# Low weight parts staged in DRAM, memory scores one unit ahead, and state space products in one pass of stacked parts

## The chip, the core and the metric

The kernel runs on one core of a Trainium2 chip. The metric is the device time of one execution in microseconds; before the change it is 2162.36 us (median of 3 runs, 2160.61 to 2164.85). A core has a matmul engine (TensorE: PE, and PEld for its weight loads), VectorE (DVE), ScalarE (ACT), GpSimd (POOL) and SyncE (SP), which here only issues DMAs. Each engine works through its own list of instructions in the order of that list, and waits on semaphores for the others; DMAs are issued from the lists of SP, ACT and POOL.

## The reference

A sequence of 512 tokens of width 1024, float32, goes through two blocks: a dilated window attention and a differential attention, each with gate and output projection; then a feed-forward network (gate and up projections of 2816, hidden product, output), a mixing layer, and a second feed-forward network. The mixing layer is where most of the change lies:

```python
q_a, k_a, v_a, q_i, k_i, w_i, u_s, q_m, gates = jnp.split(h @ w_in, offsets, axis=-1)
o_a = indexed_sparse_attention(q_a, k_a, v_a, ...) @ w_o_a      # top 128 of 512 keys per query
y_s = gelu(s5_layer(u_s, ...))                                  # 16 groups x 64 complex states
o_b = glu_a * sigmoid(glu_b)          # of y_s @ w_glu
o_m = memory_attention(q_m, m_k, m_v) @ w_o_m                   # 4 heads, 256 memory rows
g = sigmoid(gates)
x = x + (g[0] * o_a + g[1] * o_b + g[2] * o_m) @ w_out
```

The state space layer needs `bur = B_re u`, `bui = B_im u` per group (its input products), a complex linear recurrence over the 512 tokens, and `y = Re(C x) + d u`.

## The kernel before

**Weights.** All weight matrices are streamed as pieces of 128x1024 float32 (512 KB or less) through one plan, `self.plan`. A piece is loaded by SP (`_load`, L291, tile `raw`, 2 buffers), then split (`_split` L305, `split` L174): ACT casts it to the matmul's one-pass format (`wh`, L175) and DVE subtracts that from the original (`wl`, L176), the low part. A product is three one-pass matmuls, high x high, low x high and high x low (`mm3`, L151, lines L153 to L155), which together keep float32 accuracy. Split pieces have 4 buffers and are split up to three pieces ahead of use. Two shapes of loops use them: `tok` (L335, tokens on the output's partitions) and `feat` (L384, features there). Both accumulate in the four PSUM banks `pp`; a `tok` of four token tiles or a `feat` of 512 columns takes all four, so the next one can begin only when the first bank has been read out. In the feed-forward network (`ffn`, L908) the reading out of the output projection is the DVE addition `xa<-pp` (L1656).

**The order of the work.** The program is emitted by a planner that counts PE time in `self.clock`: side work is written as generators that `yield` a number of planner microseconds or a condition, and `pump` (L111) emits what is due between matmuls. Its `yield`s are guesses. What is emitted is then placed by a scheduler of the framework, engine by engine, by dependencies and its own idea of durations, so an instruction can move ahead of others that were emitted earlier. On the chip the lists that come out are fixed.

**Preparation.** While the first feed-forward runs, `prepare` (L1355) normalises the memory rows, and `s5_setup` (L966) computes the rotation tables of the state space: eight rounds on POOL (L1065 to L1067, tiles `s5cs` and `s5t`, which share the buffers `memx0` and `memx1` of the memory rows), each ended by a store to DRAM from POOL's DMA queue (L1068, `s5tab<-s5cs`). `bias_table` (L1174) makes a row `brow` (buffer `gmem`) that POOL stores as `btab`.

**Mixing.** `mix` (L1385) adds the steps: key, value and index projections, memory queries (`qm`), state space input (`us`, `ev_us` L1451), queries (`q`), then gate and output projections of the three branches (`branch`, L1498). Beside them run as generators the index search (`index_masks`, L1232, 16 rounds of MAX8 and MATCH_REPLACE8 on DVE per query tile), sparse attention (`sparse_attn`, L1267, tiles `bm`, `apt`), memory attention (`mem_attn`, L1191) and the state space (`s5_branch`, L1091). Their matmuls use plain float32 (`mm`, L158, line L159), transposes L164, PSUM banks `pa`.

Memory attention has eight units (4 token tiles x 2 pairs of heads). A unit computes scores (`pa<-mkT,qmT`), a masked row maximum on DVE and an exponential on ACT (L437, L438, tile `msm`), waits 4 planner us, transposes the probabilities (`pa<-cst,msm`) and multiplies by the values (`pa<-mv,mpt`). The next unit begins after that.

The state space has eight units too. POOL masks the input matrix to a block diagonal form (`bz`, L1125), PE transposes it, two float32 products with `us` follow (`pa<-us,bt`), then DVE and POOL rotate, scan along the tokens and rotate back (L1138 to L1154, ending with `s5t` L1153 and `s5wi` L1154); 10 planner us later PE reads them (`pa<-s5t,cz`, `pa<-s5wi,cz`).

Of the kernel before, what the change touches and what calls it, by code (L numbers as in the profile page):

```python
# [9 lines left out]
F32 = mybir.dt.float32  # L10
FR = mybir.dt.float32r
# [3 lines left out]
OP = mybir.AluOpType  # L15
# [4 lines left out]
P = 128  # L20
D = 1024
S = 512
NT = S // P
# [3 lines left out]
RAW, RING, AHEAD = 2, 4, 2  # L27
RQ = 2

S5GAP, SPGAP = 10.0, 2.5  # L30
# [35 lines left out]
class Net:  # L66
    def __init__(self, ctx, tc, consts):
        self.tc, self.nc = tc, tc.nc
        pool = lambda name, bufs, **kw: ctx.enter_context(tc.tile_pool(name=name, bufs=bufs, **kw))
        self.open = lambda c, name, bufs: c.enter_context(tc.tile_pool(name=name, bufs=bufs, reuse_waits="tile"))  # L70
        self.consts = consts
        self.cpool = pool("consts", 1)
        self.rings = {"u": pool("u", 2), "y": pool("y", 2)}
        self.wraw = pool("wraw", RAW)
        self.wsplit = pool("wsplit", RING)
        self.small = pool("small", 2)
        self.pp = pool("pp", 4, space=PSUM)
        self.pa = pool("pa", 4, space=PSUM)
        self.dram = pool("dram", 1, space=DRAM)
        self.flip = self.open_xn = 0  # L80
        self.spare_dve = False
        self.clock, self.seq, self.heap = 0.0, 0, []
        self.steps, self.plan = [], []
        self.raws, self.ready, self.live = [], {}, 0


# [204 lines left out]
    def _load(self):  # L291
# [11 lines left out]
        self.raws.append(raw)  # L303

    def _split(self):  # L305
        i = self.next_split
        raw = self.raws[i]
        n, nk = raw.shape[2], raw.shape[1]
        h, l = (self.wsplit.tile([P, 1024], FR, name="w" + x, tag="w" + x)[:, :nk * n]
                .rearrange("p (k c) -> p k c", k=nk) for x in "hl")  # L310
        self.split(raw, h, l)
        self.ready[i] = [(h[:, j, :], l[:, j, :]) for j in range(nk)]
# [778 lines left out]
    def s5_branch(self, a, us, tmp, act, dst):  # L1091
# [7 lines left out]
        tabs = []  # L1099

        def fetch(q):
            cs = tmp.tile([P, 2, S], F32, name="s5cs", tag="cs", bufs=2)
            nc.scalar.dma_start(cs, self.s5tab[q])
            tabs.append(cs)

        fetch(0)
        for ft in range(2):
# [10 lines left out]
            for qq in range(4):  # L1118
# [3 lines left out]
                bz = tmp.tile([P, 2, P], F32, name="bz", tag="bz")  # L1122
                cz = tmp.tile([P, 2, P], F32, name="cz", tag="cz")
                for i in range(2):
                    G.tensor_tensor(bz[:, i, :].rearrange("p (b c) -> p b c", c=16),  # L1125
                                    bb[:, i, q, :].unsqueeze(1).to_broadcast([P, 8, 16]), m48[:, qq], op=OP.mult)
                G.tensor_tensor(cz, ct, m4[:, qq, :].unsqueeze(1).to_broadcast([P, 2, P]), op=OP.mult)
                yield S5LEAD
                b = self.bank()
                for i in range(2):  # L1130
                    self.T(b[:, i * P:(i + 1) * P], bz[:, i, :])
                bt = tmp.tile([P, 2, P], F32, name="bt", tag="bt")
                self.evac(bt.rearrange("p i c -> p (i c)"), b[:, :2 * P])
                br, bi = self.bank(), self.bank()
                self.mm(br, bt[:, 0, :], us[:, ft, :])
                self.mm(bi, bt[:, 1, :], us[:, ft, :])
                C, Sn = (tabs[q][:, i, :] for i in range(2))
# [22 lines left out]
                nc.scalar.copy(y[rows, :], yp[rows, :])  # L1160
            yield 1.5
            t = tmp.tile([P, S], F32, name="gt", tag="t2")
            V.scalar_tensor_tensor(y, us[:, ft, :], dc[:, ft:ft + 1], y, op0=OP.mult, op1=OP.add)
            G.tensor_tensor(t, y, y, op=OP.mult)
# [25 lines left out]

    def mem_attn(self, qT, kT, v, act, at, st, bm):  # L1191
        nc = self.nc
        for t in range(NT):
            nm = st.tile([P, 4], F32, name="mnm", tag="mnm")
            den = st.tile([P, 4], F32, name="mden", tag="mden")
            o = at.tile([P, 4, 64], F32, name="mo", tag="kk", bufs=1)
            for j in range(2):
                yield bm.free
                held = bm.take()
                sm = at.tile([P, 2, 256], F32, name="msm", tag="bm", bufs=bm.n)  # L1200
                b = [self.bank()[:, :256] for _ in range(2)]
                for c in range(2):
                    hs = slice(c * 64, c * 64 + 64)
                    self.mm(b[c], qT[hs, j, t * P:(t + 1) * P], kT[hs, j, :])
                for c in range(2):
                    hd = 2 * j + c
                    self.softmax_rows(b[c], self.dm[:, :256], sm[:, c, :], nm[:, hd:hd + 1], den[:, hd:hd + 1])
                yield MEM[0]
                tb = self.bank()
                pt = at.tile([P, 4, P], F32, name="mpt", tag="apt", bufs=2)  # L1210
                for n in range(4):
                    self.T(tb[:, n * P:(n + 1) * P], sm[:, n // 2, (n % 2) * P:(n % 2 + 1) * P])
                held[0] = True
                self.evac(pt.rearrange("p n q -> p (n q)"), tb)
                po = self.bank()[:, :P]
                for c in range(2):
                    hd = 2 * j + c
                    for kt in range(2):
                        self.mm(po[:, c * 64:c * 64 + 64], pt[:, 2 * c + kt, :], v[:, kt, hd * 64:hd * 64 + 64],
                                kt == 0, kt == 1)  # L1220
                d = den[:, 2 * j:2 * j + 2]
                nc.vector.reciprocal(d, d)
                nc.vector.tensor_tensor(o[:, 2 * j:2 * j + 2, :], po.rearrange("p (h d) -> p h d", h=2),
                                        d.unsqueeze(2).to_broadcast([P, 2, 64]), op=OP.mult)
            b = self.bank()
# [3 lines left out]
            act.done.add(t)  # L1229
            yield MEM[1]  # L1230

# [123 lines left out]
    def prepare(self, a, pre, aux):  # L1355
# [15 lines left out]
        def gen():  # L1371
# [8 lines left out]
            yield 5.0  # L1380
            v["btab"] = self.bias_table(a["rel_bias"], a["onehot"], aux)

        self.co(gen())

    def mix(self, u, a, enter, merged):  # L1385
# [10 lines left out]
        def opened():  # L1396
# [7 lines left out]
            tl("qaT", [P, 4, S]), tl("kaT", [P, S]), tl("ixT", [P, 3, S]), tl("va", [P, NT, 64])  # L1404
            tl("wi", [P, NT, 4]), tl("us", [P, 2, S])
            v["M"] = [mx.tile([P, S], F32, name="M%d" % f) for f in range(KT)]
# [44 lines left out]
        def ev_us(c, ps, _):  # L1451
            self.evac(v["us"][:, c, :], ps[c])
            flags["us"].add(c)
# [37 lines left out]

        self.tok(ux, [(w, 1220, 256)], ev_heads("qm", 4, "qmT", 2), by="t")
        self.feat(ux, [(w, 964, 256)], ev_us)
        self.add(start_s5)
# [62 lines left out]
        branch(2, om, a["w_o_m"], True, False)  # L1557
        branch(1, ys, a["w_glu"], False, False)

        def leave():  # L1560
# [17 lines left out]
    def run(self, a, out):  # L1578
# [107 lines left out]
        def enter_mix():  # L1686
            self.need(lambda: len(self.mixv["mk"]) == 2)
            s3.close()
            return s2
# [122 lines left out]
```

## Time and profile before

| | |
|---|---|
| median of 3 runs | 2162.36 us (2160.61 to 2164.85) |
| profiled execution | 2165.69 us, its span 2163.9 us |
| PE busy | 2103.0 us (97%) |
| PEld busy | 1709.3 us (79%) |
| DVE busy | 1237.9 us (57%) |
| ACT busy | 938.7 us (43%) |
| POOL busy | 234.5 us (11%) |
| DMA | 204.11 MB, mean 94 GB/s |

The profile gives for each engine the time in which an instruction of it ran. PE's matmuls are pipelined: one 128x512 matmul shows some 0.39 us, but the next starts 0.23 us after it. Stages differ, so the shares of the whole span say little; the windows below cut it into stretches. The first feed-forward's weights are loaded from about 930 to 1294 us, the mixing layer's from 1327 to 1762 us. An idle stretch of an engine is shown with what ended it, and PEclk is the share of TensorE's clock that was granted.

### The profile page before, as it was taken

To read this page: it belongs to the slowest core of one execution; us is meant where nothing else is said; L and a number is where in the kernel's file an instruction comes from. 1 tells how busy PE (TensorE), PEld (TensorE's weight loads), DVE (VectorE), ACT (ScalarE), POOL (GpSimd) and SP (SyncE) were. 2 spreads that over 40 slices of the span, in tenths; PEclk is the share of its full clock that TensorE was granted. 3 is DMA by queue.
4 is the path that set the end of the run, shared out by engine and by line. 5 is a ranking of instruction groups with operands and counts; after the bars stand their busy time and mean duration, and the time that the engine had idled before them with its cause. 6 is when DMAs were issued, how large, how long until landed. Compare 5 with 4: busy or idle time off the path is not lost.

```text
span 2163.9 us, 27643 instructions
## 1 busy us (share of the span) xinstructions
PE 2103.0 (97%) x10217; PEld 1709.3 (79%) x10217; DVE 1237.9 (57%) x2673; ACT 938.7 (43%) x1885; POOL 234.5 (11%) x322
## 2 busy tenths in 40 slices
PE   7999999999999999999999999988899999999998
PEld 6888988889888776788888888755567888888887
DVE  5645457454667677876543337889885454333334
ACT  4746455464545655555223234433344234223223
POOL 0000000000000000110970000124431100000000
PEclk9999999999999999999999999989999999999999
DMA  5222222212233212233343334222243323333332
GB/s 176 88 69 69 69 70 63 83 59 69 80 127 127 88 59 69 98 120 109 117 146 98 98 98 154 79 60 74 64 143 97 110 81 99 97 97 98 98 98 78
DMA packets 152055, 204.11 MB, mean 94 GB/s; under 512 B 9848, under 2 KB 111240, under 8 KB 151920
## 3 DMA queue, kind: packets, MB, share of 16 engines
q1 hardware_dynamic: 138368, 170.70, 25.8%
q10 hardware_dynamic: 8352, 15.14, 2.4%
q0 software_dynamic: 5200, 16.50, 2.1%
q8 instruction: 80, 1.31, 0.3%
q14 instruction: 55, 0.45, 0.1%
HBM read 191.80 MB, written 10.51 MB: 93 GB/s over the span
## 4 chain that ended last, share of the span: by engine, by line
PE 49%; DVE 8%; ACT 2%; DMA 1%; issue 1%; POOL 1%; ACTq 0%; DVEq 0%; POOLq 0%; SPq 0%
PE pp L153 15%; PE pp L154 15%; PE pp L155 15%; PE pa L159 3%; PE pa L164 1%; DVE wl L176 1%; DVE s5wi L1148 1%; DVE score L1262 1%; DVE s5wr L1147 1%; DMA raw<-in_w_in 1%; ACT wh L175 1%; DVE s5t L1150 0%; ACT p L438 0%; DVE m L1261 0%; POOL s5wr L1142 0%
## 5 line engine op out<-in xcount | busy, mean ns | idle before, releaser
L176 DVE TENSOR_TENSOR wl<-raw,wh 128x1024 fp32r<-128x1024 f32 (+1 forms) x320 | 410.4, 1283 | 496.1 <-ACT wh L175 494.9
L175 ACT CAST wh<-raw 128x1024 fp32r<-128x1024 f32 (+1 forms) x320 | 333.7, 1044 | 636.8 <-PE pp L154 287.5
L153 PE MATMUL pp<-uh,wh 128*128 128x512 f32 (+1 forms) x1232 | 485.0, 394 | 0.2 <-DVE sg L445 0.2
L154 PE MATMUL pp<-ul,wh 128*128 128x512 f32 (+1 forms) x1232 | 478.2, 388 | 1.0 <-DVE ul L282 1.0
L155 PE MATMUL pp<-uh,wl 128*128 128x512 f32 (+1 forms) x1232 | 477.5, 388 | 0.0
L153 PEld LDWEIGHTS pp<-uh,wh 128*128 128x128 f32 x1232 | 232.0, 189 | 54.4 <-issue 9.9
L155 PEld LDWEIGHTS pp<-uh,wl 128*128 128x128 f32 x1232 | 232.4, 189 | 46.0 <-issue 0.6
L154 PEld LDWEIGHTS pp<-ul,wh 128*128 128x128 f32 x1232 | 233.0, 189 | 43.7 <-DVE ul L282 1.2
L153 PE MATMUL pp<-wh,uh 128*128 128x512 f32 (+2 forms) x592 | 237.9, 403 | 0.3 <-ACT wh L175 0.2
L154 PE MATMUL pp<-wl,uh 128*128 128x512 f32 (+2 forms) x592 | 229.2, 388 | 0.5 <-DVE wl L176 0.4
L155 PE MATMUL pp<-wh,ul 128*128 128x512 f32 (+2 forms) x592 | 228.6, 387 | 0.0
L153 PE MATMUL pp<-yh,wh 128*128 128x512 f32 (+1 forms) x464 | 176.0, 379 | 0.0
L154 PE MATMUL pp<-yl,wh 128*128 128x512 f32 (+1 forms) x464 | 175.1, 377 | 0.0
L155 PE MATMUL pp<-yh,wl 128*128 128x512 f32 (+1 forms) x464 | 174.8, 377 | 0.0
L425 ACT COPY rq<-pp 32x512 f32<-32x512 f32 x256 | 148.0, 578 | 58.0 <-PE pp L155 52.8
L153 PEld LDWEIGHTS pp<-wh,uh 128*128 128x128 f32 x592 | 127.8, 216 | 21.2 <-issue 4.6
L154 PEld LDWEIGHTS pp<-wl,uh 128*128 128x128 f32 x592 | 128.3, 217 | 17.3 <-DVE wl L176 1.8
L155 PEld LDWEIGHTS pp<-wh,ul 128*128 128x128 f32 x592 | 127.6, 215 | 16.6 <-issue 0.3
L153 PE MATMUL pp<-wh,yh 128*128 128x512 f32 x304 | 119.2, 392 | 0.1
L154 PE MATMUL pp<-wl,yh 128*128 128x512 f32 x304 | 118.8, 391 | 0.0
L155 PE MATMUL pp<-wh,yl 128*128 128x512 f32 x304 | 118.6, 390 | 0.0
L438 ACT ACTIVATE sm<-sm,nm 128x128 f32<-128x128 f32 (+1 forms) x192 | 79.8, 417 | 54.4 <-DVE nm L437 54.1
(404 smaller groups left out, 2774.4 us busy)
## 6 DMA issues: line engine op xcount, KB each, us to landing
raw<-in_ffn_w_in SPq DMA_DIRECT2D x176, 256.0 KB, 3.1
raw<-in_dil_w_in SPq DMA_DIRECT2D x80, 512.0 KB, 3.6
raw<-in_ffn_w_out SPq DMA_DIRECT2D x44, 512.0 KB, 3.7
raw<-in_diff_w_in SPq DMA_DIRECT2D x32, 512.0 KB, 3.7
raw<-in_w_in SPq DMA_DIRECT2D x32, 512.0 KB, 3.7
raw<-in_dil_w_out SPq DMA_DIRECT2D x8, 512.0 KB, 3.7
raw<-in_diff_w_out SPq DMA_DIRECT2D x8, 512.0 KB, 3.6
s5tab<-s5cs POOLq DMA_DIRECT2D x8, 512.0 KB, 3.3
```

Of the source, the lines that this page charges most:

```text
L153: mm(ps, a[0], b[0], start=first, stop=False)
L154: mm(ps, a[0], b[1], start=False, stop=False)
L155: mm(ps, a[1], b[0], start=False, stop=last)
L159: self.nc.tensor.matmul(ps, a, b, start=start, stop=stop)
L164: self.nc.tensor.transpose(ps, x, self.ident[:n, :n])
L175: self.nc.scalar.copy(h, src)
L176: return self.nc.vector.tensor_tensor(l, src, h.bitcast(F32), op=OP.subtract)
L425: nc.scalar.copy(sw[b:b + 32, :], ps[c][b ^ 32:(b ^ 32) + 32, :])
L438: nc.scalar.activation(sm, sm, AF.Exp, bias=nm, scale=-1.0, accum_out=den)
L1147: V.tensor_tensor_scan(wr, mag, wr, 0.0, op0=OP.mult, op1=OP.add)
L1148: V.tensor_tensor_scan(wi, mag, wi, 0.0, op0=OP.mult, op1=OP.add)
L1262: V.match_replace(sc[:, :n], m8, sc[:, :n], -BIG)
```

## The change

Three parts.

**Staging.** After the bias table and a lead of `ELEAD` = 95 planner us, a new generator `low_parts` takes the plan's pieces from the state space input on, up to the end of the second branch. For each it loads the raw weights from POOL's queue into `wr0` (the buffers `memx0` and `gmem` in turn), splits them with ACT and DVE as `_split` does (the high part goes to `wh0` in `memx1`, one buffer, and isn't kept; the low part replaces the raw data), and POOL stores the low part to DRAM (`low`). When mixing begins (`early_on` false) it stops; 21 pieces have been staged by then, 4 of them of half size. In mixing, `_split` of a staged piece casts the high part on ACT as before, and SP loads the low part instead of DVE's subtraction.

**Memory attention.** The scores of unit n + 1 are emitted before the transposes and the values of unit n; the yields become 2 and 2 planner us.

**State space input.** `us` is split into a high and a low part, which are stored to DRAM; each unit loads the 32 rows that it needs, high and low twice, stacked into 128 partitions (`u4`, four DMAs on ACT's queue). The input matrix of a unit (tile `bf`, 128x32 for real and imaginary part) is split into high and low as well, and copied by POOL into a matrix whose rows 0 to 63 hold the high part twice and 64 to 127 the low part twice (`bz`). One one-pass matmul of 128 rows then sums all four products of parts. At the end of a half the two parts of `us` are loaded again for `d u`, one addition each.

How the instructions move, in three places. First DVE, in the first feed-forward, around the copies of the bias row (`wl` is a piece's ordinary subtraction, `xa` the reading out of the output projection, `wr` a staged piece's subtraction). Before:

```order
L176 TENSOR_TENSOR wl<-raw,wh 128x1024
L1186 COPY brow<-pa 8x512
L1186 COPY brow<-pa 8x128
L176 TENSOR_TENSOR wl<-raw,wh 128x1024 x3
L1656 SCALAR_TENSOR_TENSOR xa_7835<-pp,xa_7835 128x512
L1656 SCALAR_TENSOR_TENSOR xa_7836<-pp,xa_7836 128x512
L1656 SCALAR_TENSOR_TENSOR xa_7837<-pp,xa_7837 128x512
L1656 SCALAR_TENSOR_TENSOR xa_7838<-pp,xa_7838 128x512
L176 TENSOR_TENSOR wl<-raw,wh 128x1024 x4
```

Now:

```order
L1244 COPY brow<-pa 8x512
L1244 COPY brow<-pa 8x128
L178 TENSOR_TENSOR wl<-raw,wh 128x1024 x2
L178 TENSOR_TENSOR wr_10008<-wr_10008,wh_10040 128x1024
L178 TENSOR_TENSOR wr_10043<-wr_10043,wh_10109 128x1024
L178 TENSOR_TENSOR wl<-raw,wh 128x1024
L1745 SCALAR_TENSOR_TENSOR xa_7835<-pp,xa_7835 128x512
L1745 SCALAR_TENSOR_TENSOR xa_7836<-pp,xa_7836 128x512
L1745 SCALAR_TENSOR_TENSOR xa_7837<-pp,xa_7837 128x512
L1745 SCALAR_TENSOR_TENSOR xa_7838<-pp,xa_7838 128x512
L178 TENSOR_TENSOR wr_10112<-wr_10112,wh_10158 128x1024
L178 TENSOR_TENSOR wl<-raw,wh 128x1024
```

The first two staged subtractions stand ahead of the third ordinary one and of the four additions; a third follows the additions. On ACT the casts of the same pieces stand in the same places among the ordinary casts.

Then POOL, the last table of the state space and what follows it. Before:

```order
L1066 TENSOR_TENSOR s5t<-e_8867,e_8868 128x512 x2
L1188 DMA btab<-brow 8x640
L1065 TENSOR_TENSOR s5cs<-e_8867,e_8868 128x512 x2
L1067 TENSOR_TENSOR s5cs<-s5cs,s5t 128x512 x2
L1068 DMA s5tab<-s5cs 128x1024
L1668 DMA x_82<-xa_7835 128x1024
L1668 DMA x_82<-xa_7836 128x1024
L1668 DMA x_82<-xa_7837 128x1024
```

Now:

```order
L1104 TENSOR_TENSOR s5t<-e_8867,e_8868 128x512 x2
L1246 DMA btab<-brow 8x640
L1103 TENSOR_TENSOR s5cs<-e_8867,e_8868 128x512 x2
L1105 TENSOR_TENSOR s5cs<-s5cs,s5t 128x512 x2
L1106 DMA s5tab<-s5cs 128x1024
L319 DMA wr_10043<-in_w_in 128x4x256
L319 DMA wr_10008<-in_w_in 128x4x256
L335 DMA low<-wr_10008 128x1024
L335 DMA low<-wr_10043 128x1024
L319 DMA wr_10112<-in_w_in 128x2x512
L319 DMA wr_10161<-in_w_in 128x2x512
L335 DMA low<-wr_10112 128x1024
```

The list up to the last store of a table is unchanged; the loads and stores of the staging come between it and the stores of `xa`.

Last PE, in mixing, around the products of the first state space unit (`bt` its matrix, `msm` the probabilities of a memory unit, `mkT,qmT` the scores). Before:

```order
L159 MATMUL pa<-us,bt 128x512 x2
L164 MATMUL pa<-cst,msm 128x128 x4
L153 MATMUL pp<-wh,uh 128x512
L154 MATMUL pp<-wl,uh 128x512
L155 MATMUL pp<-wh,ul 128x512
L153 MATMUL pp<-wh,uh 128x512
L159 MATMUL pa<-mv,mpt 128x64 x4
L159 MATMUL pa<-mkT,qmT 128x256 x2
```

Now:

```order
L1189 MATMUL pa<-u_11973,bt 128x512 x2
L161 MATMUL pa<-mkT,qmT 128x256 x2
L157 MATMUL pp<-wh,ul 128x512
L155 MATMUL pp<-wh,uh 128x512
L156 MATMUL pp<-wl,uh 128x512
L157 MATMUL pp<-wh,ul 128x512
L155 MATMUL pp<-wh,uh 128x512
L166 MATMUL pa<-cst,msm 128x128 x4
L156 MATMUL pp<-wl,uh 128x512
```

The scores of the second memory unit stand ahead of the transposes of the first unit's probabilities, with other matmuls between; before they came behind the first unit's values.

The diff, cut to its core (in `mem_attn` the old body is left out, and the new helpers hold the same instructions as it):

```diff
+EGAP, ELEAD = 5.0, 95.0
...
+        self.low, self.early, self.early_on = {}, (0, 0), True
...
+    def low_parts(self, pool):
+        nc = self.nc
+        yield ELEAD
+        tags = ("memx0", "gmem")
+        def load(i):
+            parts, k0, nk = self.plan[i]
+            n = sum(p[2] for p in parts)
+            r = pool.tile([P, D], F32, name="wr0", tag=tags[i % 2])[:, :nk * n].rearrange("p (k c) -> p k c", k=nk)
+            o = 0
+            for w, c0, m in parts:
+                nc.gpsimd.dma_start(r[:, :, o:o + m],
+                                    w[k0 * P:(k0 + nk) * P, c0:c0 + m].rearrange("(k p) c -> p k c", p=P))
+                o += m
+            return r
+        r = load(self.early[0])
+        for i in range(*self.early):
+            yield EGAP
+            if not self.early_on:
+                return
+            nk, n = r.shape[1], r.shape[2]
+            h = pool.tile([P, D], F32, name="wh0", tag="memx1")[:, :nk * n].rearrange("p (k c) -> p k c", k=nk)
+            self.split(r, h.bitcast(FR), r.bitcast(FR))
+            nxt = load(i + 1) if i + 1 < self.early[1] else None
+            yield EGAP / 2
+            low = self.dram.tile([P, nk, n], F32, name="low")
+            nc.gpsimd.dma_start(low, r)
+            self.low[i] = low
+            r = nxt
     def _split(self):
...
                 .rearrange("p (k c) -> p k c", k=nk) for x in "hl")
-        self.split(raw, h, l)
+        if i in self.low:
+            self.nc.scalar.copy(h, raw)
+            self.nc.sync.dma_start(l.bitcast(F32), self.low.pop(i))
+        else:
+            self.split(raw, h, l)
         self.ready[i] = [(h[:, j, :], l[:, j, :]) for j in range(nk)]
...
+        mask2 = m4[:, 0, 0:32].rearrange("p (w c) -> p w c", w=2)
+        four = {}
         def fetch(q):
...
             tabs.append(cs)
+            u4 = four[q] = tmp.tile([P, S], FR, name="u4", tag="u4", bufs=2)
+            for i in range(4):
+                nc.scalar.dma_start(u4[i * 32:i * 32 + 32, :].bitcast(F32), us[q // 4, i % 2, (q % 4) * 32:(q % 4) * 32 + 32, :])
...
                 cz = tmp.tile([P, 2, P], F32, name="cz", tag="cz")
+                z = tmp.tile([P, 2, P], F32, name="bf", tag="bt").rearrange("p i (n c) -> p (i n) c", n=4)[:, :6, :].rearrange(
+                    "p (x i) c -> p x i c", x=3)
                 for i in range(2):
-                    G.tensor_tensor(bz[:, i, :].rearrange("p (b c) -> p b c", c=16),
-                                    bb[:, i, q, :].unsqueeze(1).to_broadcast([P, 8, 16]), m48[:, qq], op=OP.mult)
+                    G.tensor_tensor(z[:, 0, i, :].rearrange("p (w c) -> p w c", w=2),
+                                    bb[:, i, q, :].unsqueeze(1).to_broadcast([P, 2, 16]), mask2, op=OP.mult)
+                zr = z.bitcast(FR)
+                V.tensor_copy(zr[:, 1], z[:, 0])
+                V.tensor_tensor(zr[:, 2], z[:, 0], z[:, 1], op=OP.subtract)
+                for i in range(2):
+                    G.tensor_copy(bz.rearrange("p i (x y c) -> p i x y c", x=2, y=2)[:, :, i],
+                                  z[:, 1 + i].unsqueeze(2).to_broadcast([P, 2, 2, 32]))
                 G.tensor_tensor(cz, ct, m4[:, qq, :].unsqueeze(1).to_broadcast([P, 2, P]), op=OP.mult)
...
                     self.T(b[:, i * P:(i + 1) * P], bz[:, i, :])
-                bt = tmp.tile([P, 2, P], F32, name="bt", tag="bt")
+                bt = tmp.tile([P, 2, P], FR, name="bt", tag="bt")
                 self.evac(bt.rearrange("p i c -> p (i c)"), b[:, :2 * P])
                 br, bi = self.bank(), self.bank()
-                self.mm(br, bt[:, 0, :], us[:, ft, :])
-                self.mm(bi, bt[:, 1, :], us[:, ft, :])
+                u4 = four.pop(q)
+                for o, i in ((br, 0), (bi, 1)):
+                    nc.tensor.matmul(o, bt[:, i, :], u4, start=True, stop=True)
+                    self.clock += 0.227
                 C, Sn = (tabs[q][:, i, :] for i in range(2))
...
                 nc.scalar.copy(y[rows, :], yp[rows, :])
-            yield 1.5
+            parts = [tmp.tile([P, S], F32, name="us" + n, tag=n) for n in ("wr", "wi")]
+            for i in range(2):
+                nc.scalar.dma_start(parts[i], us[ft, i])
+            yield 3.0
             t = tmp.tile([P, S], F32, name="gt", tag="t2")
-            V.scalar_tensor_tensor(y, us[:, ft, :], dc[:, ft:ft + 1], y, op0=OP.mult, op1=OP.add)
+            for i in range(2):
+                V.scalar_tensor_tensor(y, parts[i], dc[:, ft:ft + 1], y, op0=OP.mult, op1=OP.add)
             G.tensor_tensor(t, y, y, op=OP.mult)
...
     def mem_attn(self, qT, kT, v, act, at, st, bm):
...
+        def scores(t, j):
...
+        def rest(t, j, held, sm, o):
...
+        def out(t, o):
...
+        yield bm.free
+        now = scores(*units[0])
+        yield MEM[0]
+        for n, (t, j) in enumerate(units):
+            if j == 0:
+                o = at.tile([P, 4, 64], F32, name="mo", tag="kk", bufs=1)
+            nxt = None
+            if n + 1 < len(units):
+                yield bm.free
+                nxt = scores(*units[n + 1])
+                yield MEM[0] / 2
+            rest(t, j, *now, o)
+            now = nxt
+            yield MEM[0] / 2
+            if j == 1:
+                out(t, o)
...
             v["btab"] = self.bias_table(a["rel_bias"], a["onehot"], aux)
+            yield from self.low_parts(aux)
...
-            tl("wi", [P, NT, 4]), tl("us", [P, 2, S])
+            tl("wi", [P, NT, 4])
...
         def ev_us(c, ps, _):
-            self.evac(v["us"][:, c, :], ps[c])
+            if c == 0:
+                v["us"] = self.dram.tile([2, 2, P, S], F32, name="us")
+            h, l = (v["s5t"].tile([P, S], FR, name="us" + n, tag=n) for n in (("t1", "t2"), ("wr", "wi"))[c])
+            self.split(ps[c], h, l)
+            for i, z in enumerate((h, l)):
+                nc.scalar.dma_start(v["us"][c, i], z.bitcast(F32))
             flags["us"].add(c)
...
         self.tok(ux, [(w, 1220, 256)], ev_heads("qm", 4, "qmT", 2), by="t")
+        first = len(self.plan)
         self.feat(ux, [(w, 964, 256)], ev_us)
...
         branch(1, ys, a["w_glu"], False, False)
+        self.early = (first, len(self.plan))
...
             self.need(lambda: len(self.mixv["mk"]) == 2)
+            self.early_on = False
             s3.close()
```

## Rows read from the trace of the kernel before

**Rows 1.** windows: stretch, length, busy PE PEld DVE ACT POOL, PEclk, DMA, GB/s
```profile
1000.00:1100.00 100.00, 99.89 (x444) 81.28 (x442) 51.44 (x47) 27.24 (x33) 70.58 (x135) 1.00 0.37 119
...
1200.00:1300.00 100.00, 100.00 (x443) 82.81 (x442) 35.76 (x39) 25.68 (x30) 0.00 (x0) 1.00 0.32 95
...
1400.00:1500.00 100.00, 86.63 (x372) 57.46 (x371) 89.56 (x209) 39.09 (x88) 39.23 (x37) 0.93 0.21 61
...
1500.00:1600.00 100.00, 83.82 (x345) 55.52 (x344) 87.97 (x159) 33.10 (x88) 43.48 (x41) 0.93 0.32 90
```

**Rows 2.** waits of PE, 1380 to 1700: total us, times, longest
```profile
PE pa L164 <- ACT msm L438: 11.6, 8, 2.2
...
PE pa L164 <- DVE anm L437: 4.3, 1, 4.3
...
PE pa L159 <- DVE s5t L1153: 2.6, 2, 2.0
```

**Rows 3.** windows again, 20 us around the longest wait of rows 2
```profile
1520.00:1540.00 20.00, 14.88 (x48) 9.21 (x49) 14.02 (x29) 5.25 (x15) 4.05 (x6) 0.83 0.29 68
```

**Rows 4.** timeline of DVE: start, us, what, xcount [idle before]
```profile
1085.57 1.39 DVE L176 TENSOR_TENSOR wl<-raw,wh 128x1024 fp32r<-128x1024 f32 x1 [4.14 <-ACT wh L175]
...
1091.01 1.75 DVE L176 TENSOR_TENSOR wl<-raw,wh 128x1024 fp32r<-128x1024 f32 x1 [4.05 <-ACT wh L175]
...
1092.68 2.02 DVE L1656 SCALAR_TENSOR_TENSOR xa<-pp,xa 128x512 f32<-128x512 f32 x3
...
1095.37 0.69 DVE L1656 SCALAR_TENSOR_TENSOR xa<-pp,xa 128x512 f32<-128x512 f32 x1 [0.67 <-PE pp L155]
```

**Rows 5.** timeline of PE, last matmul of one group, first of the next
```profile
1094.94 0.39 PE L155 MATMUL pp<-wh,yl 128*128 128x512 f32 x1
...
1095.16 0.39 PE L153 MATMUL pp<-uh,wh 128*128 128x512 f32 x1
```

**Rows 6.** timeline of ACT, casts of two weight pieces
```profile
1084.48 1.06 ACT L175 CAST wh<-raw 128x1024 fp32r<-128x1024 f32 x1 [4.38 <-PE pp L155]
...
1089.92 1.06 ACT L175 CAST wh<-raw 128x1024 fp32r<-128x1024 f32 x1 [4.38 <-PE pp L155]
```

**Rows 7.** timeline of POOL, tables of the state space
```profile
1077.63 0.60 POOL L1068 DMA_DIRECT2D s5tab<-s5cs  x1 [0.30 <-POOL s5cs L1067]
...
1083.34 2.54 POOL L1067 TENSOR_TENSOR s5cs<-s5cs,s5t 128x512 f32<-128x512 f32 x2
...
1086.18 0.60 POOL L1068 DMA_DIRECT2D s5tab<-s5cs  x1 [0.30 <-POOL s5cs L1067]
...
1091.64 3.53 POOL L1067 TENSOR_TENSOR s5cs<-s5cs,s5t 128x512 f32<-128x512 f32 x2
...
1123.74 0.60 POOL L1068 DMA_DIRECT2D s5tab<-s5cs  x1 [0.30 <-POOL s5cs L1067]
```

**Rows 8.** DMA issues: xcount, KB each, median us to landing
```profile
s5tab<-s5cs POOLq DMA_DIRECT2D x8, 512.0 KB, 3.3
...
raw<-in_w_in SPq DMA_DIRECT2D x32, 512.0 KB, 3.7
...
memx<-in_mem POOLq DMA_DIRECT2D x2, 512.0 KB, 4.5
```

**Rows 9.** timeline of PE, products of state space unit 1, next instruction
```profile
1393.18 1.98 PE L159 MATMUL pa<-us,bt 128*128 128x512 f32 x4 [1.00 <-ACT bt L170]
...
1395.00 0.60 PE L164 MATMUL pa<-cst,msm 128*128 128x128 f32 x4
```

**Rows 10.** timelines of PE and DVE, unit 2: products, last rotation step
```profile
1416.39 1.99 PE L159 MATMUL pa<-us,bt 128*128 128x512 f32 x4
...
1428.47 0.68 DVE L1153 TENSOR_TENSOR s5t<-s5t,s5t 128x512 f32<-128x512 f32 x1
```

**Rows 11.** groups by line and form, 1300 to 1700: xcount | busy, mean ns
```profile
L176 DVE TENSOR_TENSOR wl<-raw,wh 128x1024 fp32r<-128x1024 f32 x40 | 52.9, 1323 | 28.5 <-ACT wh L175 28.4
...
L176 DVE TENSOR_TENSOR wl<-raw,wh 128x512 fp32r<-128x512 f32 x4 | 2.8, 703 | 0.5 <-ACT wh L175 0.5
```

More of the change, by code (lines that the diff above doesn't have):

```diff
@@ L1192, in mem_attn @@
         nc = self.nc
[L1193 to L1224, printed above, removed]
@@ new lines, in mem_attn @@
+        rows = {}
+        units = [(t, j) for t in range(NT) for j in range(2)]
+        def scores(t, j):
+            if j == 0:
+                rows[t] = (st.tile([P, 4], F32, name="mnm", tag="mnm"), st.tile([P, 4], F32, name="mden", tag="mden"))
+            nm, den = rows[t]
+            held = bm.take()
+            sm = at.tile([P, 2, 256], F32, name="msm", tag="bm", bufs=bm.n)
+            b = [self.bank()[:, :256] for _ in range(2)]
+            for c in range(2):
+                hs = slice(c * 64, c * 64 + 64)
+                self.mm(b[c], qT[hs, j, t * P:(t + 1) * P], kT[hs, j, :])
+            for c in range(2):
+                hd = 2 * j + c
+                self.softmax_rows(b[c], self.dm[:, :256], sm[:, c, :], nm[:, hd:hd + 1], den[:, hd:hd + 1])
+            return held, sm
@@ new lines, in rest @@
+        def rest(t, j, held, sm, o):
+            tb = self.bank()
+            pt = at.tile([P, 4, P], F32, name="mpt", tag="apt", bufs=2)
+            for n in range(4):
+                self.T(tb[:, n * P:(n + 1) * P], sm[:, n // 2, (n % 2) * P:(n % 2 + 1) * P])
+            held[0] = True
+            self.evac(pt.rearrange("p n q -> p (n q)"), tb)
+            po = self.bank()[:, :P]
+            for c in range(2):
+                hd = 2 * j + c
+                for kt in range(2):
+                    self.mm(po[:, c * 64:c * 64 + 64], pt[:, 2 * c + kt, :], v[:, kt, hd * 64:hd * 64 + 64],
+                            kt == 0, kt == 1)
+            d = rows[t][1][:, 2 * j:2 * j + 2]
+            nc.vector.reciprocal(d, d)
+            nc.vector.tensor_tensor(o[:, 2 * j:2 * j + 2, :], po.rearrange("p (h d) -> p h d", h=2),
+                                    d.unsqueeze(2).to_broadcast([P, 2, 64]), op=OP.mult)
@@ L1229, in mem_attn @@
             act.done.add(t)
-            yield MEM[1]
+        yield bm.free
+        now = scores(*units[0])
+        yield MEM[0]
+        for n, (t, j) in enumerate(units):
+            if j == 0:
+                o = at.tile([P, 4, 64], F32, name="mo", tag="kk", bufs=1)
[9 more added lines that the diff above has]
+                out(t, o)
     def index_masks(self, ixT, wi, at, st, masks):
```

## The prediction

> **What bounds the kernel now.** I read the times first, then the windows of 100 us, then TensorE's waits, then the timelines of the two places that the change touches. TensorE bounds nearly the whole program. In the first feed-forward it is never idle: 443 matmuls in 100 us are one per 0.226 us, and POOL's 70 us in the window before are the state space tables, beside everything else [rows 1]. The exception is the mixing stage. From 1400 to 1600 us PE is busy 86.6 and 83.8 of 100, so 29.6 us idle, with VectorE at 89.6 and 88.0: two engines that wait for each other. The granted clock there is 0.93, so 2 x 7 = 14 us more go to stretches at 1.2 instead of 2.4 GHz. The largest single wait is the transpose of the memory probabilities for ACT's exponential (11.6 us in eight waits); the state space rotation costs only 2.6 [rows 2]. One 4.3 us wait is followed by a window of 20 us at 0.83 (3.4 us lost), which shows how idle time brings the clock down [rows 3].
>
> So there are at most some 44 us to win in mixing, and every microsecond for which the feed-forward stops PE is paid in full, since nothing there has slack to catch up.
>
> **Staging: the feed-forward.** The lead of 95 planner us only says where the staging is emitted; the scheduler then moves each instruction to where its inputs are ready by its own reckoning. In the new order ACT's cast and DVE's subtraction of the first two staged pieces stand two ordinary subtractions behind the copies of the bias row. In the trace of before that place is after the subtraction at 1085.57 and before the one at 1091.01, which is followed by the four additions `xa<-pp` (from 1092.68) [rows 4]; on ACT it is between the casts at 1084.48 and 1089.92 [rows 6]. Each engine works its list in order. The data come from POOL, whose new loads stand behind the last `s5tab` store, and POOL issues that store only at 1123.74 [rows 7]. Up to the first staged instruction the lists of all engines are the same as before, so these times carry over: ACT and DVE will stand still at about 1087 for data whose DMA isn't issued before about 1121.
>
> Who waits behind them: the additions `xa<-pp` free the four accumulator banks, and the next `feat` needs the first of them at 1095.16, directly after the last matmul of the group before [rows 5]. PE stops there. When does it go on?
> - POOL. Its last store at 1123.74 was reached in rounds that DVE disturbed: the two subtractions of a table took 2.54 us in one round and 3.53 in another [rows 7]. An undisturbed round is 1086.18 - 1077.63 = 8.55 us; four of them and 0.6 us for issuing the bias store, from 1086.18 on, give 1121.0. So 1121.0 to 1123.7.
> - The load reuses the table's buffer, so it waits for that store to land: 3.3 us. A load of 512 KB lands in 3.7 (a weight piece) to 4.5 us (`memx`, from POOL) [rows 8]. Data at 1128.0 to 1131.5.
> - Then one after the other, since both staged pieces share one buffer for the high part: cast 1.06, subtraction 1.39, cast 1.06, subtraction 1.39, the ordinary subtraction 1.39, the first addition 0.69 [rows 4, 6]: 7.0 us. PE goes on at 1135.0 to 1138.5, that is 39.8 to 43.3 us after 1095.16. I take 41.5.
>
> The Trainium skill (SBUF — State Buffer, section "Who interferes with whom") says that a DVE instruction with two SBUF inputs and a GpSimd one that reads SBUF lock each other out; with DVE standing still that rule alone would give the early end, 39.8, and without it the late one, 43.3. The 2.54 and 3.53 us agree with the rule.
>
> After it two smaller terms. PE comes back from a long idle; by the loss after the 4.3 us wait I add 2.5 us (0 to 5) for the clock [rows 3]. The other 19 staged pieces follow about one for each ordinary piece. Two of them take store 3.3, load 4.5, cast 1.06, subtraction 1.39, about 10.3 us, against 2 x 5.44 us of matmuls per two ordinary pieces (1085.57 to 1091.01), so they nearly keep step: 2 us (0 to 8). Cost of the staging together: 46 us, ends 40 and 56. DMA has room (share 0.32 to 0.37 [rows 1]); were the queues in each other's way, the load would take longer and so would the stall.
>
> **Mixing: what comes back.**
> - Products of the state space: two plain float32 products take 1395.00 - 1393.18 = 1.82 us [rows 9], the one-pass ones 2 x 0.226. Eight units save 8 x 1.37 = 11 us of PE.
> - Memory: transposes now follow the scores of the next unit, not their own. Of 11.6 us I take 8 back (0 to 11.6).
> - VectorE: 17 subtractions at 1.32 us and 4 at 0.70 go, 25 us [rows 11], of which all but the first three, some 21 us, lie in the stretch that waits; two low parts of `us` and two additions of 128x512 come (0.69 each, as in [rows 4]) and sixteen instructions of an eighth of that size, which I estimate at 0.2 us each: 6 us. Net -15 us on an engine at 89%. It shortens PE's other waits, 29.6 - 11.6 - 2.6 = 15.4 us; I take 4 (0 to 15), since DVE stays close to full.
> - The low parts now come by SP, 3.7 us each, three ordinary pieces ahead of their use (16 us): nothing. If this cover goes, as among the short pieces of `w_o_m`, one wait is 2 us.
> - Clock: 4 of the 14 us (0 to 14).
> - New wait. From the start of the products to the rotated state is 1429.15 - 1416.39 = 12.8 us (start of the subtraction plus 0.68) [rows 10]; shorter products make it 11.4. Counted in the order with the durations above, PE's work between product and `s5t` sums to 96 us over eight units before and 77 now, since the products shrink and the first is pushed back by its four small loads. Needed are 8 x 11.4 = 91: 14 short, where before 8 x 12.8 = 102 were 6 short and showed 2.6. I charge 9 us (0 to 25). The forty DMA issues that ACT gains lie in its idle time (busy 39 and 33 of 100 [rows 1]) and count in this range.
>
> Sum: -11 - 8 - 4 - 4 + 9 = -18 us, ends -40 and +8.
>
> **The sum.** The profiled execution took 2165.7 us. 2165.7 + 46 - 18 = 2193.7; it stood 3.3 us above the median of 2162.4, so by the median the forecast is 2190 us.
>
> **Rivals.**
> 1. The staging doesn't block: the change does what its lead says and the pieces come late enough. For it: the lead of 95 us, and POOL is idle from 1124. Against it: the order, in which no instruction of POOL's tables moved. Then only mixing counts: 2162 - 18 + 2 = 2146 us, faster. It decides if the first staged cast waits under 18 us. Chance 0.08.
> 2. The stall comes, and the state space chain takes all that mixing gains: PE stops before `s5t` some 3 us in each of eight units and the clock falls with it. For it: 14 us short in the count. Against: DVE with less work shortens the chain. 2162 + 46 + 3 = 2211 us. Chance 0.17.
> 3. The stall comes, and mixing loses most of its idle time (-38): 2162 + 46 - 38 = 2170. For it: two engines that wait for each other both lose work. Against: DVE at 89% gives up only 15 of some 178 us. Chance 0.15.
> The forecast has 0.60, with a range of its own of 2176 to 2204.
>
> About 0.2%, 4 us, is what a measurement of this kernel can tell from no change. Only rival 1 is faster (0.08); some 0.02 lies within 0.2%, where the low ends of stall and mixing meet; 0.90 is slower. The range for 8 in 10, 2167 to 2208, leaves out rival 1 and the upper half of rival 2.
>
> **What would show it.** In the profile after: PE idle for some 41 us from about 1095 before a `pp` matmul, put down to DVE's `xa`; ACT and DVE idle from about 1087, ended by the DMA of `wr`; POOL's last table store at 1121 to 1124. In mixing: `msm` waits under 4 us, `s5t` waits of 9 us or more, two products in 0.45 us, DVE some 15 us less busy. It is wrong if the feed-forward shows no such gap, or if mixing changes by more than 40 us either way.

## The result and the profile after

The changed kernel takes 2217.6 us (median of 4, 2213.6 to 2219.7) against 2163.6 before: slower, ratio 1.0244 (95% interval 1.0229 to 1.0259). The forecast was 2190 us with a range to 2208. The way and the place were right, the size of one step was not.

The profiled execution took 2213.6 us (span 2211.9; before 2163.9). The windows of the first feed-forward, whose PE was busy without a break before [rows 1], with the columns of that group:

```profile
1000.00:1100.00 100.00, 93.31 (x411) 75.48 (x409) 42.85 (x37) 23.68 (x28) 72.41 (x138) 0.98 0.34 111
1100.00:1200.00 100.00, 59.64 (x240) 48.36 (x241) 34.66 (x35) 27.91 (x32) 32.06 (x42) 0.78 0.61 201
1200.00:1300.00 100.00, 90.33 (x377) 73.39 (x376) 37.94 (x41) 27.46 (x33) 12.34 (x19) 0.95 0.49 157
```

PE is idle for 56.7 us there and the clock falls; from 1100 us on the DMA share is 0.61 and 0.49, where it was 0.32 to 0.37. PE's waits, 1085 to 1300 us (total, times, longest):

```profile
PE pp L155 <- DVE xa L1745: 37.4, 1, 37.4
PE pp L155 <- DVE sg L962: 14.9, 3, 6.6
PE pp L155 <- ACT sg L961: 4.3, 2, 2.9
```

The first line is the forecast stall. The 19.2 us under it weren't forecast. The timeline of ACT and DVE shows the cause of the first:

```profile
1124.29 1.04 ACT L177 CAST wh<-wr 128x1024 fp32r<-128x1024 f32 x1 [40.66 <-DMA wr<-in_w_in]
...
1125.36 1.23 DVE L178 TENSOR_TENSOR wr<-wr,wh 128x1024 fp32r<-128x1024 f32 x1 [40.20 <-ACT wh L177]
...
1129.98 2.48 DVE L1745 SCALAR_TENSOR_TENSOR xa<-pp,xa 128x512 f32<-128x512 f32 x4
```

Both engines stood for 40 us before the first staged piece, with the additions `xa` behind it [rows 4]. POOL's timeline in the same place:

```profile
1116.30 0.60 POOL L1106 DMA_DIRECT2D s5tab<-s5cs  x1 [0.30 <-POOL s5cs L1105]
1116.90 0.79 POOL L319 DMA_DIRECT2D wr<-in_w_in  x1
1119.60 0.76 POOL L319 DMA_DIRECT2D wr<-in_w_in  x1 [1.91 <-DMA s5tab<-s5cs]
...
1130.08 0.72 POOL L319 DMA_DIRECT2D wr<-in_w_in  x1 [0.30 <-DMA low<-wr]
...
1207.09 0.71 POOL L319 DMA_DIRECT2D wr<-in_w_o_m  x1 [4.46 <-DMA low<-wr]
```

The loads follow the last table store at 1116.3. From 1130.08 to 1207.09 twelve more go out, one in 6.42 us, and nearly each waits for the store of a low part.

To split the difference I use two VectorE instructions that both kernels have. The one on `xa` ahead of the feed-forward starts at 964.16 before and at 962.25 after, 1.9 us earlier:

```profile
964.16 1.41 DVE L490 SCALAR_TENSOR_TENSOR xa<-acc,rstd,xa 128x512 f32<-128x512 f32 x2
```
```profile
962.25 1.41 DVE L528 SCALAR_TENSOR_TENSOR xa<-acc,rstd,xa 128x512 f32<-128x512 f32 x2
```

The feed-forward's last addition stands before at

```profile
1327.13 0.68 DVE L1656 SCALAR_TENSOR_TENSOR xa<-pp,xa 128x512 f32<-128x512 f32 x1
```

and after, 65.3 us later, at

```profile
1392.39 0.68 DVE L1745 SCALAR_TENSOR_TENSOR xa<-pp,xa 128x512 f32<-128x512 f32 x1
```

So the feed-forward costs 65.3 + 1.9 = 67.2 us, and the rest of the program gives back 65.3 - 48.0 = 17.3 us. The forecast had 46 and 18. The two profiled executions are 48.0 us apart, the medians 54; where the other 6 us lie is not shown. In the mixing stage, PE's waits (1340 to 1760 us, the longest) answer [rows 2]:

```profile
PE pa L161 <- ACT apt L172: 4.6, 5, 1.6
PE pa L161 <- DVE s5t L1207: 4.4, 2, 3.1
PE pa L166 <- ACT bm L476: 4.4, 3, 2.3
PE pa L161 <- ACT mpt L172: 3.2, 2, 1.9
```

The 11.6 us before `msm` are gone; `mpt`, `bm` and `s5t` have grown. All waits from the last addition to the end of the program sum to 29.5 us, against 32.2 before. Two products now stand as one row in PE's timeline:

```profile
1462.66 0.63 PE L1189 MATMUL pa<-u,bt 128*128 128x512 f32 x2
```

### The profile page after: what moved, and what is told of

It is laid out like the page before. It is cut to its first block, busy times and chain, and to the rows that moved or that the text cites. A ratio compares the mean times of both kernels' runs of the same rounds, so it can differ in the third digit from the quotient of the medians.

```text
span 2211.9 us, 27858 instructions
## 1 busy us (share of the span) xinstructions
PE 2098.2 (95%) x10201; PEld 1709.2 (77%) x10201; DVE 1235.9 (56%) x2693; ACT 956.0 (43%) x1906; POOL 252.6 (11%) x382
## 5 line engine op out<-in xcount | busy, mean ns | idle before, releaser
L178 DVE TENSOR_TENSOR wl<-raw,wh 128x1024 fp32r<-128x1024 f32 (+1 forms) x299 | 382.0, 1278 | 451.1 <-ACT wh L177 449.7
L177 ACT CAST wh<-raw 128x1024 fp32r<-128x1024 f32 (+1 forms) x299 | 313.2, 1048 | 567.8 <-PE pp L156 240.1
L155 PE MATMUL pp<-uh,wh 128*128 128x512 f32 (+1 forms) x1232 | 488.6, 397 | 52.3 <-DVE xa L1745 37.4
```

Of the source, the lines that this page charges most:

```text
L155: mm(ps, a[0], b[0], start=first, stop=False)
L177: self.nc.scalar.copy(h, src)
L178: return self.nc.vector.tensor_tensor(l, src, h.bitcast(F32), op=OP.subtract)
```

## The experiments

Below, "feed-forward" is what a kernel loses or gains between these two instructions and "rest" what it does after them, against the kernel before, each in one profiled execution; ratios are over all runs of a kernel, against the kernel before on the same chip. One execution is not the mean of all: on one chip, 19 runs of the kernel before went from 2161.6 us (mean granted clock 0.995) to 2171.3 (0.989), so a few us in "rest" say little.

**1. The mixing edits without the staging**

```diff
-            yield from self.low_parts(aux)
```

> The changed kernel without the staging: memory scores one unit ahead and one-pass state space products alone. Theory A (the staging costs 67 us in the feed-forward, and of the 17 us won in mixing most come from products and memory): no gap at 1095 us, 2148 to 2156 us. Theory B (the mixing gain is the relief of VectorE, whose 21 subtractions are gone there): with the subtractions back the gain shrinks to under 5 us, 2159 us or more.

2166.5 us, ratio 1.0002 (0.9993 to 1.0011): no gain at all (feed-forward -0.3, rest -0.4). My theory A was wrong on mixing; the number is B's: without the staging nothing is left of 17 us. Whether B's reason is right, the next run tells.

**2. The staging alone**, added to the kernel before with the same code as in the change.

> The kernel before with the staging alone. Theory A: 67 us lost in the feed-forward, some 5 us back in mixing, 2218 to 2231 us. Theory B: 17 us back in mixing, 2205 to 2217 us. In both a PE gap of 35 to 42 us after 1095 us.

2234.3 us, 1.0315 (1.0301 to 1.0329), above both. Feed-forward +69.8, rest +0.7: the relief alone gives nothing either. Neither A nor B holds on mixing.

**3. Two staged pieces instead of 21**

```diff
-        self.early = (first, len(self.plan))
+        self.early = (first, first + 2)
```

> The changed kernel with 2 staged pieces instead of 21. Theory A (the first two pieces cost the 37 us gap, the other 19 the rest, since a staged piece takes longer than an ordinary one): the gap stays at 35 to 40 us, the stalls of 3 to 7 us after it go, 2184 to 2199 us. Rival C (the losses after the gap are its own aftermath: a backlog and a clock that comes back slowly): they stay, 2208 us or more.

2205.0 us, 1.0178 (1.0164 to 1.0192), between the two; the trace tells them apart:

```profile
PE pp L155 <- DVE xa L1745: 38.0, 1, 38.0
```

That is all of PE's waiting between 1085 and 1300 us, and the whole feed-forward loses 39.4 us. So the gap costs 38 us and under 2 us of clock, and it has no aftermath: C is out. The other 67.2 - 39.4 = 28 us come from the 19 later pieces. (The total is 6 us above A's range; with two pieces the rest gains nothing, +1.1 us.)

**4. The same loads and stores, without the casts and subtractions**

```diff
-            h = pool.tile([P, D], F32, name="wh0", tag="memx1")...
-            self.split(r, h.bitcast(FR), r.bitcast(FR))
```

> The changed kernel with all 21 staged loads and stores, but without their casts and subtractions (the raw weights are stored in the place of the low parts, so this computes something else). Theory A (ACT and DVE stand in line behind a staged piece; the transfers themselves harm nobody): no gap of over 5 us in the feed-forward, 2146 to 2156 us. Rival D (the transfers, DMA share up to 0.87, hold up the feed-forward's own weights): 20 us or more of the loss stay, 2170 us or more.

2149.8 us, 0.9924 (0.9911 to 0.9938): faster than before. The window of the feed-forward, 1100 to 1300 us:

```profile
1100.00:1300.00 200.00, 200.00 (x884) 165.64 (x884) 72.14 (x73) 53.60 (x64) 49.77 (x62) 1.00 0.64 209
```

PE is busy throughout at a DMA share of 0.64, above that of the changed kernel. The transfers by themselves harm nobody (D is out); what costs is ACT and DVE standing in line.

**5. The low parts made but not stored** (mixing makes them itself, as before)

```diff
-            low = self.dram.tile([P, nk, n], F32, name="low")
-            nc.gpsimd.dma_start(low, r)
-            self.low[i] = low
```

> The changed kernel whose 21 staged low parts are made but not stored, so mixing makes them itself as before. Theory A (the pace after the gap is that of two buffers that wait for store and load, 6.55 us a piece against 5.44): without stores the buffers come free earlier, the 28 us after the gap shrink to under 8 and the gap stays: 2166 + 38 + 0 to 8 = 2204 to 2213 us. Rival F (what stalls is the place of the staged casts in the lists of ACT and DVE, whatever the buffers do): the 28 us stay, 2225 us or more.

2214.5 us, 1.0225 (1.0209 to 1.0242). The waits, 1085 to 1300 us:

```profile
PE pp L155 <- DVE xa L1742: 36.9, 1, 36.9
PE pp L155 <- DVE sg L959: 3.3, 2, 2.5
PE pp L155 <- ACT sg L958: 2.8, 2, 2.1
```

19.2 us of waits after the gap shrink to 6.1. The feed-forward loses 46.6 us, so its loss after the gap (39.4 by experiment 3) goes from 28 to 7 us. The lists didn't stay the same: after the first pieces the scheduler now places about two staged pieces for each ordinary one, where the changed kernel has one, and a staged cast comes every 3.4 us. So the staged casts stand closer in the lists of ACT and DVE than before, and yet cost less: F is out, and it is the buffers' round through the store that made the pieces slow, theory A. (Its total lies 1.5 us above A's range.)

**6. The staged casts and subtractions held at their written place**

```diff
-            self.split(r, h.bitcast(FR), r.bitcast(FR))
+            keep = self.tc.keep_in_program_order
+            keep(nc.scalar.copy(h.bitcast(FR), r))
+            keep(nc.vector.tensor_tensor(r.bitcast(FR), r, h, op=OP.subtract))
```

> The changed kernel with the casts and subtractions of the 21 staged pieces held at their place in the written order, so that the first stands some 16 ordinary pieces later. Theory A (all the loss is instructions that stand in line ahead of their data): the gap at 1095 us goes; since the staged pieces still follow each other one for one ordinary piece, up to 15 us of small stalls stay: 2150 to 2165 us. Rival E (the staging costs ACT and DVE too much wherever it stands): 2185 us or more.

2151.3 us, 0.9939 (0.9922 to 0.9956): faster than both kernels. Feed-forward -0.2, rest -14.6. PE has no wait between 1085 and 1300 us. The first staged subtraction now stands 18 ordinary ones behind the bias row, 16 later than in the change, and the cast before it finds its data landed (no idle time is shown):

```profile
1172.87 1.04 ACT L332 CAST wh<-wr 128x1024 fp32r<-128x1024 f32 x1
```

E is out: the same 21 pieces cost nothing there. But the edit changes more than the place: in the written order the staged pieces stand two for three ordinary ones, not one for one as I expected, and come one in 8.6 us in the feed-forward, slower than the 6.42 that their buffers allowed. It fits that no small stalls are left, but this run alone doesn't tell place and pace apart.

**7. Held, earlier and more: lead 45, 28 pieces**

```diff
-EGAP, ELEAD = 5.0, 95.0
+EGAP, ELEAD = 5.0, 45.0
```

> The same with a lead of 45 and 7.5 between pieces: 28 staged pieces. If VectorE's relief sets the mixing gain, seven more pieces give 3 to 8 us more: 2141 to 2148 us. If mixing is held by its chains of waits by now, nothing more: 2148 to 2154 us. If the pace is too fast: above 2154 us.

2155.8 us, 0.9957 (0.9943 to 0.9970). Feed-forward +10.2, rest -20.7. The first cast again stands ahead of its data:

```profile
1131.48 1.05 ACT L332 CAST wh<-wr 128x1024 fp32r<-128x1024 f32 x1 [12.61 <-DMA wr<-in_w_in]
```

and PE waits once:

```profile
PE pp L155 <- ACT sg L963: 6.9, 1, 6.9
```

That wait ends at 1146.00 with `sg`, which stands on ACT right behind a later staged cast:

```profile
1144.41 1.04 ACT L332 CAST wh<-wr 128x1024 fp32r<-128x1024 f32 x1 [3.85 <-DMA wr<-in_w_in]
```

It is a smaller dose of the same; between the two staged casts an ordinary load came 4.1 us late as well, so the 6.9 us are not put down to one of them.

Two more settings of the same constants, lead 45 with 9 planner us a piece (21 pieces), and lead 65 with 7 (26 pieces):

> The same with a lead of 45 instead of 95 planner us and 9 instead of 7.5 between pieces: 21 staged pieces, two for about three ordinary ones. Theory A: a staged piece comes less often than its buffers allow, no stall in the feed-forward, the mixing gain of 14 to 17 us stays: 2147 to 2154 us. Rival E: 2185 us or more.

2158.8 us, 0.9961 (0.9949 to 0.9974): PE has no wait in the feed-forward, though ACT stood 9.3 us before the first staged cast, and the staged pieces stand one for two ordinary ones. But the rest is only -10.5, so the total lies above A's range.

> The changed kernel with staged pieces in their written place, a lead of 65 and 7 planner us a piece: 26 pieces. If mixing gains some 1.2 us more for each further piece (14.6 us with 21, 23.2 with 28) and the first piece finds its data landed: no stall, 2166 - 20 = 2146 us (2143 to 2149). If the pace of 7 us is too fast: 2150 us or more.

2154.4 us, 0.9946 (0.9932 to 0.9960): feed-forward +0.6, rest -10.3, so the rule of 1.2 us a piece failed. (Its 23.2 us for 28 pieces were taken at a later instruction; at the two used here they are 20.7.) None of the three beat experiment 6; why 21 pieces gave 14.6 and 10.5 us, and 26 pieces less than 28, is open.

**8 to 11. Which mixing edit pays.** Experiment 6 without the new products, then without the new memory order; then each edit alone, without staging. Where the memory order is the old one, the products enter the planner's clock at their old cost, so that it plans as before:

```diff
-                    self.clock += 0.227
+                    self.clock += 0.86
```

> The kernel before with the new memory order and 21 staged pieces in their written place (lead 95), with the old state space products. Theory H (with VectorE relieved, the memory wait of 11.6 us is the limit that matters): half or more of the 15 us stays without the new products, 2151 to 2159 us. Theory G (the relief pays only when the products are short as well): under 5 us, 2161 us or more.

2166.0 us, 1.0005 (0.9996 to 1.0014): G. Feed-forward -0.5, rest +4.5.

> The kernel before with the new state space products (entered in the planner at their old cost) and the same staging, with the old memory order. Theory H: the memory wait stays and eats the shorter products, 2160 us or more. Theory G': the products' 11 us come through whole once VectorE is relieved, 2151 to 2157 us.

2152.7 us, 0.9944 (0.9928 to 0.9959): G'. H, the guess that the memory wait is the limit, fell.

> The kernel before with the new state space products alone (entered in the planner at their old cost): no staging, old memory order. Theory J (products and relief pay only together, since VectorE sets the pace of mixing until it is relieved): 2162 us or more. Theory K (the products pay by themselves, and the new memory order is what took their gain back in the kernel without staging): 2151 to 2157 us.

2160.7 us, 0.9978 (0.9969 to 0.9988), between J and K.

> The kernel before with the new memory order alone. Theory J: the wait of 11.6 us goes and comes back as others, 2162 to 2168 us. Theory K: the order costs what the products gain, 2171 us or more. By the forecast's own term: 8 us less, 2157 us.

2169.3 us, 1.0020 (1.0009 to 1.0032): the old wait is gone and some 4 to 6 us are lost (rest +6.3). Neither J nor K alone. The waits of this kernel that took its place (1340 to 1760 us):

```profile
PE pa L159 <- ACT apt L170: 6.5, 3, 4.1
PE pa L164 <- DVE ao L1357: 5.6, 1, 5.6
PE pa L159 <- ACT mpt L170: 5.4, 2, 4.8
PE pa L159 <- DVE s5t L1153: 4.8, 2, 3.3
PE pa L164 <- DVE yl L964: 4.4, 1, 4.4
```

To see where the products' gain goes, one window of 320 us over each kernel's mixing, in this order: before, after (moved by 65 us), mixing edits without staging, products alone, memory order alone, staging and products, and last the two that have the relief with the old products, staging alone (moved by 70 us) and staging with the memory order:

```profile
1340.00:1660.00 320.00, 287.67 (x1341) 205.31 (x1340) 262.75 (x632) 131.02 (x313) 102.82 (x98) 0.96 0.32 91
```
```profile
1405.00:1725.00 320.00, 290.68 (x1414) 213.09 (x1413) 251.31 (x640) 137.83 (x328) 98.38 (x114) 0.97 0.45 139
```
```profile
1340.00:1660.00 320.00, 283.21 (x1328) 207.47 (x1327) 263.67 (x652) 131.31 (x315) 102.05 (x113) 0.93 0.37 105
```
```profile
1340.00:1660.00 320.00, 285.58 (x1368) 206.92 (x1367) 265.60 (x656) 134.30 (x320) 109.03 (x114) 0.95 0.36 105
```
```profile
1340.00:1660.00 320.00, 285.65 (x1311) 204.28 (x1310) 264.00 (x625) 126.84 (x303) 97.47 (x96) 0.94 0.30 88
```
```profile
1340.00:1660.00 320.00, 283.51 (x1395) 207.44 (x1394) 247.59 (x642) 137.51 (x330) 105.22 (x119) 0.98 0.48 144
```
```profile
1410.00:1730.00 320.00, 289.95 (x1343) 207.79 (x1342) 247.35 (x610) 130.41 (x313) 100.18 (x98) 0.95 0.41 122
```
```profile
1340.00:1660.00 320.00, 288.33 (x1316) 207.05 (x1315) 245.70 (x609) 128.45 (x306) 97.73 (x99) 0.94 0.41 128
```

Read PEclk: 0.01 is 3.2 us here. With the sum of PE's waits from the last addition on (32.2 us before) a balance can be made: products (-11, the forecast's estimate) + change of the waits + change of the clock, against the measured rest:

| kernel | waits | balance | rest |
|---|---|---|---|
| after | 29.5 | -11 - 2.7 - 3.2 = -17 | -17.3 |
| mixing edits, no staging | 36.9 | -11 + 4.7 + 9.6 = +3 | -0.4 |
| products alone | 35.2 | -11 + 3.0 + 3.2 = -5 | -6.9 |
| memory order alone | 35.7 | 3.5 + 6.4 = +10 | +6.3 |
| staging and products | 37.3 | -11 + 5.1 - 6.4 = -12 | -12.2 |

It closes to within 4 us. The relief of VectorE (263 to 266 us busy without staging, 246 to 251 with it) shortens the waits by 7 us at most; the larger part comes from the clock: with the new products 0.93 and 0.95 without the relief, 0.97 and 0.98 with it. With the old products it stays at 0.95 and 0.94 (the last two windows) though VectorE is relieved as much.

The mean clock of whole executions, over all runs, agrees; there 0.001 is some 2 us. It is 0.992 to 0.993 in the kernel before, 0.989 to 0.991 in the four kernels that don't stall and lack the staging or the products (experiments 1, 8, 10 and 11), and 0.994 to 0.995 with both (experiments 6 and 9). So the clock rises only where relief and products stand together; those four kernels lie below the kernel before. Of the three settings after experiment 6, 28 and 26 pieces had 0.994 and the lead of 45 with 21 pieces only 0.992. Why, stays open: no run changed the clock by itself.

## Why the prediction was wrong

**Right.** The stall, by its mechanism: ACT and DVE ahead of their data, `xa` behind them, PE without a free bank. Forecast 41.5 us, measured 37.4; the clock after it, 2.5 forecast, is under 2 by experiment 3. The 4 us are POOL's: I took rounds of 8.55 us, but with DVE standing they took 1108.30 - 1100.47 = 7.83:

```profile
1100.47 0.60 POOL L1106 DMA_DIRECT2D s5tab<-s5cs  x1 [0.30 <-POOL s5cs L1105]
...
1103.49 2.06 POOL L1103 TENSOR_TENSOR s5cs<-e,e 128x512 f32<-128x512 f32 x2 [0.33 <-DMA s5tab<-s5cs]
...
1108.30 0.60 POOL L1106 DMA_DIRECT2D s5tab<-s5cs  x1 [0.30 <-POOL s5cs L1105]
```

The round that I called undisturbed was not: in the kernel before, a DVE subtraction at 1080.13 (1.30 us) ran beside its pair `s5cs<-e,e`, which took 2.73 us where the same pair takes 2.06 above:

```profile
1080.65 2.73 POOL L1065 TENSOR_TENSOR s5cs<-e,e 128x512 f32<-128x512 f32 x2 [0.31 <-DMA s5tab<-s5cs]
```

The rule of the Trainium skill (SBUF — State Buffer, section "Who interferes with whom") pointed the right way, and the rounds agree with it. It accounts for less of the early end than the prediction says: of the 3.5 us between 39.8 and 43.3, the rounds are 2.7, and 0.8 is the choice of a load of 3.7 instead of 4.5 us. No run varied DVE alone, so it stays an agreement.

**The step that failed**: "The other 19 staged pieces follow about one for each ordinary piece. Two of them take ... about 10.3 us ... so they nearly keep step: 2 us (0 to 8)." Measured: 28 us, 19.2 of them waits and the other 9 the clock that falls with them (0.94 from 1140 to 1300 us, last section). The page gives the landing times of loads and stores:

```profile
wr<-in_w_in POOLq DMA_DIRECT2D x17, 512.0 KB, 4.8
low<-wr POOLq DMA_DIRECT2D x17, 512.0 KB, 4.7
```

I took the store from a quiet stretch, 3.3 us [rows 8], and left out what lies between the four steps. One buffer's round is load 4.8, cast 1.04, subtraction 1.23 and store 4.7, 11.8 us; the issuing is included (the load issued at 1119.60 is cast at 1124.29, 4.7 us later). Two buffers would give a piece in 5.9 us; 6.42 was seen, which is a round of 12.8, so about 1 us a round is left for the hand-overs and for waiting in POOL's own list (0.30 us from the landing of a store to the next load, in the row at 1130.08). The ordinary pieces come in 5.44. Since the lists hold one for one, the ordinary pieces fall to the slower pace: 19 x (6.42 - 5.44) = 18.6 us as an estimate, against 19.2 us of waits. Experiment 5, which takes the store out of the round, brings the 28 down to 7. So the round of 10.3 us that should "nearly keep step" with 10.9 was one of 12.8, and each of 19 pieces paid for it; that such waits also bring the clock down, the term had not counted at all.

**Mixing** came out in sum (-18 forecast, -17.3 measured), but that is luck: most of its terms were off. The products' own time was right (two showed 1.98 us [rows 9] and show 0.63), yet alone they gave 4.7 us and not 11. The memory order, -8, is worth nothing and alone costs some 4 us: a wait removed from one of two engines that wait for each other came back before `apt`, `ao`, `mpt` and `s5t`. The relief, -4, gives nothing alone and some 7 us with the products (0.9978 to 0.9944), much of it by the clock. `s5t` grew from 2.6 to 4.4 us, not by 9. The waits as a whole were forecast at -3 (-8 - 4 + 9) and gave -2.7, by cancelling. The ends of the sum, -40 and +8, are also narrower than those of its terms, which add up to -52 and +14.

Rival 1 (no blocking, 2146 us) didn't happen, but experiment 6 makes it happen with one edit, and 2151 us is then close to what it gave.

## What to carry to other kernels

Work "hidden" on an in-order engine is hidden only if its data are there when its turn comes: held behind the real arrival (here 16 pieces later, and at two pieces for three ordinary ones) the same work cost nothing. For repeated side work compare its round through its buffers, with loads and stores at their loaded durations, with the pace of what it is mixed with; the difference is paid once per piece. And test each edit in the presence and the absence of the others: here staging and products together gave 12 us where the products alone gave 5 and the staging alone none, and the memory order paid nowhere.

## What the runs showed of the hardware

The same 512 KB store from POOL's queue landed in 3.1 us with two staged pieces (experiment 3), in 4.7 with 21:

```profile
low<-wr POOLq DMA_DIRECT2D x2, 512.0 KB, 3.1
```

Copying 21 pieces beside the feed-forward at a DMA share of 0.64 (experiment 4) cost PE nothing, though the share had been 0.32 to 0.37.

And a stall of 38 us cost little clock afterwards (under 2 us), while five of 1.4 to 6.6 us came with some 9 us lost to the clock. In experiment 3, from the end of the gap on, then in the changed kernel, from soon after it, PEclk is the third number from the end:

```profile
1132.00:1300.00 168.00, 168.00 (x736) 138.99 (x736) 56.89 (x62) 42.90 (x50) 0.00 (x0) 0.99 0.32 99
```
```profile
1140.00:1300.00 160.00, 140.78 (x584) 114.22 (x583) 63.22 (x67) 48.33 (x57) 24.09 (x37) 0.94 0.59 189
```

Here several short gaps were dearer in clock than one long one.
